# The first convolution block at 512 columns with single k-tiles first, attention's two roundings in another order, and a copy of the last gate/up block's transposed products

## The chip, the cores and the metric

The kernel runs on one core of a Trainium2 chip. The metric is device time in microseconds of that core for one execution; a smaller number is better. The core has a matrix engine, TensorE (PE), three engines for element work, VectorE (DVE), ScalarE (ACT) and GpSimd (POOL), and SyncE (SP), which here only issues transfers. The engines have an instruction stream each and wait for one another through semaphores. Transfers are issued by SP, ACT or POOL and run on 16 DMA engines. TensorE writes into PSUM, a small memory apart from SBUF, which the other engines read from.

## The reference

One layer of a hybrid block for 256 rows of 2048 numbers, all in float32. `x` is normalized, a single projection of 5120 columns gives the queries, keys and values of four attention heads and the two inputs of a convolution branch, both branches are joined and projected, and a SwiGLU network follows:

```python
xn = rms_norm(h, norm1_g[l])
proj = jnp.einsum('bsd,dn->bsn', xn, w_in[l])
q, k, v, ga, gg = jnp.split(proj, ...)                  # 1024 columns each
q = apply_rope(rms_norm(q, q_norm_g[l]), cos, sin)      # and k likewise
att = diff_attention(q, k, v, lam)                      # softmax 0 - lam * softmax 1, block-causal
att = rms_norm(att, subln_g[l]) * (1.0 - lambda_init)
u = ga * jax.nn.sigmoid(gg)
u = causal_depthwise_conv(u, conv_w[l], conv_b[l])      # 1024 channels, 31 taps
u = jax.nn.silu(layer_norm(u, conv_ln_g[l], conv_ln_b[l]))
mixed = jnp.concatenate([att, u], axis=-1)
h = h + jnp.einsum('bsm,md->bsd', mixed, w_out[l])
hn = rms_norm(h, norm2_g[l])
a = jnp.einsum('bsd,df->bsf', hn, w_gate[l])            # 5632 columns
bu = jnp.einsum('bsd,df->bsf', hn, w_up[l])
h = h + jnp.einsum('bsf,fd->bsd', jax.nn.silu(a) * bu, w_down[l])
```

## The kernel before, in words

**Operands.** The 256 rows are two row tiles of 128 (`m`), and the 2048 input columns of a projection are 16 k-tiles of 128. Every float32 operand is split in two: a high part rounded to the matrix engine's narrower type (`lhi`, `whi`, made on ACT) and what is left over (`llo`, `wlo`, made on DVE). A product is then three matmuls, high times high (L377), low part of the rows times high part of the weights (L378), and high part of the rows times low part of the weights (L383). The gate, up and down projections go the same way (L1085 to L1087, L1106, L1107 and L1111), most of them in a scheme that computes seven block products in place of eight.

**Chunks.** Weights come in chunks of 1024 numbers for each of 128 partitions, 512 KB: as a rule two k-tiles of a block of 512 columns, or four k-tiles of a block of 256 columns. SP loads a chunk as `raw` (`load_chunk`, L329), ACT casts `whi` (`round_chunk`, L338), DVE subtracts `wlo` (`split_chunk`, L347), and PE multiplies (`multiply`). For some chunks the low part is made without DVE: ACT writes minus `raw`, and a transfer issued by POOL adds the weights to it in flight (`wlo` at L341 and L342, or `lod` at L333 and L334 in `minus_chunk`). The planner `run_chunks` (from L466) writes the code chunk by chunk. Before the multiplication of chunk t it emits loads, casts and subtractions of the chunks that follow, as far ahead as the constants `AHEAD`, `ROUND_AHEAD` and `MINUS_AHEAD` say. The order of the code is the order in each engine's stream. `before` is a table of things to emit ahead of a chunk's load: transfers of the transposed input (`x_load`, L157), of the plain input (`h_load`, L517), and the constants.

**Beside the chunks.** Work that comes after a block is a generator, which is resumed twice for every chunk, and whose `yield` and `lag(n)` set how many half chunks lie between its steps. `room` and `held` count the four PSUM buffers called `aux` that these generators share; the blocks' sums have four of their own (`acc`). The convolution's taps are a queue by themselves (`side`): each half chunk emits as many taps (L593, one multiply-add on DVE of 128x256) as a credit of 1.30 us allows, out of which other work on DVE is paid too.

**Order of the work.** (1) At the start 19 transposes of an identity keep PE busy (`warm_up`), ACT issues the transfers of the gains (`cols`, a table with one row for each partition) and of the first two k-tiles of `x`, SP those of weights and of the rest. `x_part` makes `lhi` and `llo` for each k-tile of `x` by `split_scaled` (L239 on ACT, L240 on DVE), scaled with the gain of that k-tile. (2) The convolution's blocks come first: two of 256 columns (one channel tile of 128 with its gate), then three of 512 columns. The first block's chunks follow the parts of `x` (`XPARTS`, here 2, 2, 4, 4 and 4 k-tiles). The third block's sums lie in two buffers of the `aux` set (`spare`). After each of them `glu_done` waits for the row norms (`normed`, out of `h`), takes the sigmoid on ACT, makes `u` on DVE, transposes it on PE (`ps_u`), copies it to `upad` on ACT and puts 30 taps for each channel tile in the side queue. (3) Keys, queries and values follow, with `qk_rows` and `attend_scores` beside them (`p` at L767 is scaled by `a`, which POOL makes at L758 from a reciprocal of DVE's). `v_done` copies the values out of PSUM (L791), and `attend_values` makes for each of four heads `ps_o` on PE, `att` on ACT (L818), the transposes `ps_at` on PE (L826) and then `mahi` and `malo` for both column halves. (4) When all taps of four channel tiles are done, `conv_back` transposes them (`ps_y`, L614), copies them back, and, after the second half, normalizes them on ACT and transposes again (`ps_ln`, L652). (5) The output projection, which reads `mahi`, `malo` and the convolution's parts. (6) The SwiGLU network in three groups of gate/up blocks with their down blocks. After a gate/up block `transposed` (from L932) transposes the products, 256 columns at a time, to `ps_a` (L917), and makes high and low parts of them (L948 on ACT, L950 on DVE). After the last such block, number 10, come the down blocks of the last group, which read its parts.

## Time and profile before

| | |
|---|---|
| median of 3 runs | 1044.78 us (1044.53 to 1044.81) |
| the profiled execution's own time | 1043.19 us |
| its span in the trace | 1041.0 us |
| PE busy | 1030.0 us, 4739 instructions |
| PE's weight loads busy | 854.7 us |
| DVE busy | 864.5 us, 1088 instructions |
| ACT busy | 685.1 us, 865 instructions |
| POOL busy | 157.4 us, 197 instructions |
| granted TensorE clock | 1.0 |
| moved by DMA | 258.06 MB, mean 248 GB/s |

The span runs from the first to the last recorded event; the execution's own time is 2.2 us longer. Busy time is the time in which an engine worked on an instruction; weight loads (PEld) go beside matmuls. Matmuls are pipelined and their ends are modelled, so the rows of single matmuls overlap: from one start to the next is their real step. A row of the timeline gives the time from the start of the span, the busy time, the engine, the line in the code, the operation, output and inputs, shapes, the count of like instructions in a row, and in brackets the idle time before it with what ended it. In the list of waits stand the engine that waited, for which instruction, on whom, and then the total, the number of waits and the longest.

### The profile page before, as it was taken

The numbers are of one execution on the slowest core, as the hardware profiler recorded it, in microseconds if no ns is written. First come the engines' busy times: TensorE is split into PE (matmuls) and PEld (weight loads), VectorE is DVE, ScalarE is ACT, GpSimd is POOL, SyncE is SP. The second block draws the span as 40 slices with busy tenths as digits, with TensorE's granted clock in tenths as the row PEclk, the third lists the DMA queues.
The fourth block names the chain that finished last, engine by engine and source line by source line (L and its number), as shares of the span: only waits on it lengthen the run. The fifth ranks groups of instructions, "written<-read, shape, count | busy, mean of one in ns | idle before, by whom it ended". The sixth has DMA issues, their size and how long they took to land.

```text
span 1041.0 us, 13235 instructions
## 1 busy us (share of the span) xinstructions
PE 1030.0 (99%) x4739; PEld 854.7 (82%) x4739; DVE 864.5 (83%) x1088; ACT 685.1 (66%) x865; POOL 157.4 (15%) x197
## 2 busy tenths in 40 slices
PE   8999999999999999999999999999999999999998
PEld 8888888887788888788888888888888888888786
DVE  5799989996546599999979689998896697998983
ACT  6855567857756567777656567776765666767661
POOL 0130134322110101011002120110101121001121
PEclk9999999999999999999999999999999999999999
DMA  9776867675566669898889998987979999889896
GB/s 361 277 205 227 258 184 205 197 206 155 188 182 233 227 217 284 232 328 241 260 238 294 269 308 265 306 236 245 303 201 270 306 272 327 236 249 301 241 252 134
DMA packets 65346, 258.06 MB, mean 248 GB/s; under 512 B 7424, under 2 KB 8448, under 8 KB 57856
## 3 DMA queue, kind: packets, MB, share of 16 engines
q1 hardware_dynamic: 48224, 201.34, 53.4%
q0 software_dynamic: 16768, 55.58, 28.0%
q8 instruction: 37, 0.61, 0.2%
q10 hardware_dynamic: 288, 0.29, 0.1%
q14 instruction: 29, 0.24, 0.1%
HBM read 248.80 MB, written 8.39 MB: 247 GB/s over the span
## 4 chain that ended last, share of the span: by engine, by line
PE 94%; ACT 2%; DVE 1%; issue 1%; DMA 1%; POOL 1%; SPq 0%; DVEq 0%; ACTq 0%
PE q L1106 11%; PE q L1107 11%; PE q L1111 11%; PE acc L383 11%; PE acc L378 11%; PE acc L377 11%; PE q L1085 9%; PE q L1087 8%; PE q L1086 8%; PE ps_a L917 1%; DMA raw<-in_wts_dram 1%; ACT whi L338 1%; PE ps_s L728 1%; PE ps_h L854 0%; PE ps_qk L713 0%
## 5 line engine op out<-in xcount | busy, mean ns | idle before, releaser
L338 ACT CAST whi<-raw 128x1024 fp32r<-128x1024 f32 (+1 forms) x261 | 270.7, 1045 | 105.7 <-PE acc L378 46.3
L347 DVE TENSOR_TENSOR wlo<-raw,whi 128x1024 fp32r<-128x1024 f32 (+1 forms) x173 | 209.4, 1216 | 76.5 <-ACT whi L338 76.5
L377 PE MATMUL acc<-whi,lhi 128*128 128x512 f32 (+1 forms) x448 | 167.4, 379 | 1.6 <-ACT whi L338 1.2
L378 PE MATMUL acc<-whi,llo 128*128 128x512 f32 (+1 forms) x448 | 165.7, 375 | 0.9 <-DVE llo L240 0.9
L1068 DVE TENSOR_TENSOR wl<-wt,wh 128x2048 fp32r<-128x2048 f32 x58 | 132.6, 2287 | 20.1 <-ACT wh L1063 20.1
L1059 ACT CAST wh<-wb 128x1536 fp32r<-128x1536 f32 x58 | 86.0, 1483 | 87.1 <-PE q L1086 42.8
L342 POOL DMA_DIRECT2D wlo<-in_wts_dram x74 | 65.0, 889 | 510.7 <-ACT wlo L341 482.6
L1106 PE MATMUL q<-whi,chi 128*128 128x512 f32 x320 | 124.7, 390 | 0.0
L1107 PE MATMUL q<-whi,clo 128*128 128x512 f32 x320 | 124.6, 389 | 0.0
L1063 ACT CAST wh<-wt 128x2048 fp32r<-128x2048 f32 x58 | 110.4, 1904 | 18.6 <-DVE wt L1054 18.6
L1085 PE MATMUL q<-wh,fhi 128*128 128x512 f32 x280 | 109.1, 390 | 0.4 <-DVE sum L1190 0.4
L1087 PE MATMUL q<-wl,fhi 128*128 128x512 f32 x280 | 109.0, 389 | 0.0
L1086 PE MATMUL q<-wh,flo 128*128 128x512 f32 x280 | 108.9, 389 | 0.0
L1067 DVE TENSOR_TENSOR wl<-wb,wh 128x1536 fp32r<-128x1536 f32 x58 | 101.6, 1751 | 2.1 <-ACT wh L1059 2.1
L593 DVE SCALAR_TENSOR_TENSOR y<-upad,cw,y 128x256 f32<-128x256 f32 x240 | 101.9, 484 | 0.6 <-ACT y L586 0.4
L383 PE MATMUL acc<-wlo,lhi 128*128 128x512 f32 (+1 forms) x404 | 101.9, 377 | 0.0
L377 PEld LDWEIGHTS acc<-whi,lhi 128*128 128x128 f32 x448 | 84.4, 188 | 17.1 <-ACT whi L338 1.6
L378 PEld LDWEIGHTS acc<-whi,llo 128*128 128x128 f32 x448 | 84.4, 188 | 16.0 <-DVE llo L240 1.1
L1111 PE MATMUL q<-wlo,chi 128*128 128x512 f32 x320 | 86.9, 393 | 0.0
L383 PEld LDWEIGHTS acc<-wlo,lhi 128*128 128x128 f32 x404 | 71.5, 189 | 12.7
L341 ACT ACTIVATE wlo<-raw 128x1024 fp32r<-128x1024 f32 x74 | 78.1, 1056 | 0.0
L1052 DVE TENSOR_TENSOR wt<-wb 128x1024 f32<-128x1024 f32 x58 | 70.8, 1220 | 0.8 <-DMA wb<-in_wts_dram 0.4
(216 smaller groups left out, 1733.1 us busy)
## 6 DMA issues: line engine op xcount, KB each, us to landing
raw<-in_wts_dram SPq DMA_DIRECT2D x259, 512.0 KB, 5.8
wb<-in_wts_dram SPq DMA_DIRECT2D x57, 1024.0 KB, 8.1
wlo<-in_wts_dram POOLq DMA_DIRECT2D x74, 512.0 KB, 9.5
lod<-in_wts_dram POOLq DMA_DIRECT2D x14, 512.0 KB, 6.9
out_dram<-sum POOLq DMA_DIRECT2D x22, 256.0 KB, 7.0
h<-in_x_dram SPq DMA_DIRECT2D x4, 512.0 KB, 9.5
out_dram<-h POOLq DMA_DIRECT2D x8, 256.0 KB, 3.7
xt<-in_xt_dram SPq DMA_DIRECT2D x3, 512.0 KB, 7.3
```

The lines of the kernel that those rows point to most:

```text
L338: act.copy(c["hi"], c["raw"])
L347: dve.tensor_tensor(c["lo"], c["raw"], c["hi"].bitcast(F32), ALU.subtract)
L377: pe.matmul(ps[m], xhi[:, ms], hi[:, j, :], start=c["first"] and j == 0, stop=False)
L378: pe.matmul(ps[m], xlo[:, ms], hi[:, j, :], start=False, stop=False)
L383: pe.matmul(ps[m], xhi[:, ms], lo[:, j, :], start=False, stop=c["last"] and j == nk - 1)
L1068: dve.tensor_tensor(c["lo"][:, :4], c["t"], c["hi"][:, :4].bitcast(F32), ALU.subtract)
L1085: pe.matmul(ps, fhi[:, f, p, :], c["hi"][:, w], start=bool(first), stop=False)
L1086: pe.matmul(ps, flo[:, f, p, :], c["hi"][:, w], start=False, stop=False)
L1087: pe.matmul(ps, fhi[:, f, p, :], c["lo"][:, w], start=False, stop=bool(last))
L1106: pe.matmul(ps, plain[i][0][:, ms], hi[:, i, :], start=i == 0 and bool(c["first"].get(qs[m])), stop=False)
L1107: pe.matmul(ps, plain[i][1][:, ms], hi[:, i, :], start=False, stop=False)
L1111: pe.matmul(sum_bank(c, qs[m]), plain[i][0][:, ms], lo[:, i, :], start=False, stop=i == 1 and bool(c["last"].get(qs[m])))
```

## The change

There are five edits.

First, the convolution's blocks are four of 512 columns, where two of 256 and three of 512 columns stood. `XPARTS` has nine parts, of 1, 1 and seven times 2 k-tiles, so the first block's nine chunks are two of one k-tile (256 KB) and seven of two. No block's sums lie in the `aux` buffers any more, and `spare` leaves `glu_done`.

Second, the gains lie in the rows of the transposed input: each partition's row begins with its 58 gains, then come the 16 k-tiles. ACT's first transfer, `head`, brings the gains and k-tile 0 together, its second brings k-tile 1, and POOL copies the gains into `cols`. The parts of k-tiles 0 and 1 are scaled by gains read from `head`. `head` lies in the memory of `lod`.

Third, what stands around it moves: 17 warm-up transposes for 19, transfers of `h` from the load of the sixth chunk on (`H_FROM`) between those of `x`, late constants behind the load of the eleventh, and the count from which `minus_chunk` is used begins at 8 for 12, as the first block has more chunks.

Fourth, `attend_values` emits both roundings `mahi` on ACT and then both `malo` on DVE, where the code had `mahi` and `malo` of one column half ahead of those of the other, and two half chunks lie between `att` and the transposes for one. `v_done` begins one half chunk sooner.

Fifth, for gate/up block 10 `transposed` first copies the transposed products from PSUM into a tile `ac` on ACT, and both parts are made from the copy.

On SP at the start of the program, before, weights (`raw`) and parts of the transposed input (`xt`) alternate, and the plain input (`h`) follows behind all of `xt`. From the fourth load of weights to the constants:

```order
L329 DMA raw<-in_wts_dram 128x1024
L157 DMA xt<-in_xt_dram 128x1024
L329 DMA raw<-in_wts_dram 128x1024
L517 DMA h_81<-in_x_dram 128x1024
L329 DMA raw<-in_wts_dram 128x1024
L517 DMA h_82<-in_x_dram 128x1024
L329 DMA raw<-in_wts_dram 128x1024
L517 DMA h_81<-in_x_dram 128x1024
L329 DMA raw<-in_wts_dram 128x1024
L517 DMA h_82<-in_x_dram 128x1024
L329 DMA raw<-in_wts_dram 128x1024 x2
```

Now each `xt` is half as large, and the transfers of `h` stand between the last of them. The last two of each, to the constants:

```order
L159 DMA xt<-in_xt_dram 128x512
L521 DMA h_81<-in_x_dram 128x1024
L333 DMA raw<-in_wts_dram 128x1024
L159 DMA xt<-in_xt_dram 128x512
L521 DMA h_82<-in_x_dram 128x1024
L333 DMA raw<-in_wts_dram 128x1024 x5
L180 DMA cw<-in_conv_w_dram 128x248
L182 DMA gb<-in_vecs_dram 128x256
```

The ninth load of weights is the first of the last row of `raw` in both pieces, and all of `xt` and `h` stands ahead of it before as after. What moved is `h`, in between the last parts of `xt`, and the constants, which stand behind the tenth load of weights before and behind the thirteenth now.

On DVE at the start, before, low parts of `x` come two or four at a time between those of the weights:

```order
L240 SCALAR_TENSOR_TENSOR llo<-xt,cols,lhi 128x256 x2
L347 TENSOR_TENSOR wlo<-raw,whi 128x512 x2
L240 SCALAR_TENSOR_TENSOR llo<-xt,cols,lhi 128x256 x2
L347 TENSOR_TENSOR wlo<-raw,whi 128x1024
L240 SCALAR_TENSOR_TENSOR llo<-xt,cols,lhi 128x256 x4
L347 TENSOR_TENSOR wlo<-raw,whi 128x1024
L240 SCALAR_TENSOR_TENSOR llo<-xt,cols,lhi 128x256 x4
L347 TENSOR_TENSOR wlo<-raw,whi 128x1024
```

Now one each for the first two chunks (`head` holds k-tile 0 and the gains), and then two:

```order
L244 SCALAR_TENSOR_TENSOR llo<-head,lhi 128x256
L351 TENSOR_TENSOR wlo<-raw,whi 128x512 x2
L244 SCALAR_TENSOR_TENSOR llo<-xt,head,lhi 128x256
L351 TENSOR_TENSOR wlo<-raw,whi 128x1024
L244 SCALAR_TENSOR_TENSOR llo<-xt,cols,lhi 128x256 x2
L351 TENSOR_TENSOR wlo<-raw,whi 128x1024
L244 SCALAR_TENSOR_TENSOR llo<-xt,cols,lhi 128x256 x2
L351 TENSOR_TENSOR wlo<-raw,whi 128x1024
```

On ACT where attention's values of the first two heads are done, before: `att` of head 0, its two `mahi`, `att` of head 1, a cast of weights, and `mahi` of head 1.

```order
L818 ACTIVATE att<-ps_o,ro 128x256 x2
L239 ACTIVATE mahi<-ps_at,cols 128x256 x2
L818 ACTIVATE att<-ps_o,ro 128x256 x2
L338 CAST whi<-raw 128x1024
L239 ACTIVATE mahi<-ps_at,cols 128x256 x2
L767 ACTIVATE p_2555<-pr,a_2491 128x128
L767 ACTIVATE p_2557<-pr,a_2495 128x256
L338 CAST whi<-raw 128x1024
```

Now `att` of head 1 comes ahead of the roundings of head 0, and a cast stands between `att` and `mahi` of either:

```order
L820 ACTIVATE att<-ps_o,ro 128x256 x2
L342 CAST whi<-raw 128x1024
L820 ACTIVATE att<-ps_o,ro 128x256 x2
L832 ACTIVATE mahi<-ps_at,cols 128x256 x2
L342 CAST whi<-raw 128x1024
L832 ACTIVATE mahi<-ps_at,cols 128x256 x2
L770 ACTIVATE p_2441<-pr,a_2379 128x128
L770 ACTIVATE p_2443<-pr,a_2383 128x256
L342 CAST whi<-raw 128x1024
```

From the gate and up projections on, the streams of all engines are the same but for the copies. On ACT at the last gate/up block, before:

```order
L1063 CAST wh<-wt 128x2048
L948 CAST lhi<-ps_a 128x512
L338 CAST whi<-raw 128x1024
L341 ACTIVATE wlo<-raw 128x1024
L948 CAST lhi<-ps_a 128x512
L1059 CAST wh<-wb 128x1536
L338 CAST whi<-raw 128x1024 x2
```

Now a copy stands ahead of each cast, and the cast reads the copy:

```order
L1072 CAST wh<-wt 128x2048
L955 COPY ac<-ps_a 128x512
L957 CAST lhi<-ac 128x512
L342 CAST whi<-raw 128x1024
L345 ACTIVATE wlo<-raw 128x1024
L955 COPY ac<-ps_a 128x512
L957 CAST lhi<-ac 128x512
L1068 CAST wh<-wb 128x1536
L342 CAST whi<-raw 128x1024 x2
```

No other row moved there; DVE's low parts, in the same places as before, read `ac`. What moved is the moment at which `ps_a` is read for the last time: at DVE's low part before, at ACT's copy now.

The diff:

```diff
--- before.py
+++ after.py
@@ -49,18 +49,20 @@
 
 NK = 2
 
-WARM = 19
-
-XPARTS = (range(0, 2), range(2, 4), range(4, 8), range(8, 12), range(12, 16))
-
-CONV_BLOCKS = (1, 1, 2, 2, 2)
+WARM = 17
+
+XPARTS = (range(0, 1), range(1, 2)) + tuple(range(k, k + 2) for k in range(2, 16, 2))
+
+CONV_BLOCKS = (2, 2, 2, 2)
+
+H_FROM = 5
 
 AHEAD = 2
 ROUND_AHEAD, MINUS_AHEAD = 3, 5
 RAW_BUFS = 4
 AUX = 4
 
-MINUS_FROM = 12
+MINUS_FROM = 8
 
 LAG = (3, 2, 6)
 HL_BUFS = 4
@@ -113,7 +115,7 @@
 def tile_block(
     ctx: ExitStack,
     tc: tile.TileContext,
-    x, xt, conv_w, gains, vecs, rope, wts, out, placed_at,
+    x, xt, conv_w, vecs, rope, wts, out, placed_at,
 ):
     nc = tc.nc
     PSUM = bass.MemoryType.PSUM
@@ -155,10 +157,12 @@
         i, k = divmod(ks[0], HK)
         n = len(ks)
         queue.dma_start(out=halves_of_x[i][:, k : k + n].rearrange("p k s -> p (k s)"),
-                        in_=xt[:, ks[0] * S : (ks[0] + n) * S])
-
-    act.dma_start(out=cols, in_=gains)
-    x_load(XPARTS[0], act)
+                        in_=xt[:, NR + ks[0] * S : NR + (ks[0] + n) * S])
+
+    head = pre.tile([P, NK * N], F32, tag="lod", name="head", bufs=1)[:, : NR + S]
+    act.dma_start(out=head, in_=xt[:, : NR + S])
+    x_load(XPARTS[1], act)
+    pool.tensor_scalar(cols, head[:, :NR], 1.0, 0.0, ALU.mult, ALU.add)
 
     act.copy(small.tile([P, 8], F32, tag="rsq", name="first"), neghalf)
 
@@ -522,7 +526,8 @@
     def x_part(ks):
         for k in ks:
             xT[k] = lhs_pair("x", k)
-            split_scaled(xT[k], halves_of_x[k // HK][:, k % HK], col("g1", k))
+            src = halves_of_x[k // HK][:, k % HK] if k else head[:, NR:]
+            split_scaled(xT[k], src, col("g1", k) if k > 1 else head[:, AT["g1"] + k : AT["g1"] + k + 1])
 
     def x_rest():
         for part in XPARTS[1:]:
@@ -554,7 +559,7 @@
         pool.memset(upad[b][:, :, : W - 1], 0.0)
     y = pre.tile([P, NCT, S], F32, tag="y", name="y", bufs=1)
 
-    def glu_done(c0, nct, ps, spare):
+    def glu_done(c0, nct, ps):
 
         w = nct * P
         while not normed:
@@ -570,8 +575,6 @@
             u = pre.tile([P, HN], F32, tag="wt", name="u", bufs=4)
             dve.scalar_tensor_tensor(u[:, :w], ps[m][:, w:], rstd1[m], sig[m][:, :w], ALU.mult, ALU.mult)
             us.append(u)
-        if spare:
-            held[0] -= NM
         spend(0.25)
         yield from lag(4 if c0 == 0 else 3)
         yield from room(1)
@@ -786,7 +789,6 @@
         wTs[hd] = wT
 
     def v_done(b, ps):
-        yield
         for m in range(NM):
             act.activation(v_sb[m][:, b * N : (b + 1) * N], ps[m], AF.Copy, scale=rstd1[m])
         yield
@@ -818,16 +820,19 @@
             act.activation(at_, o[:, m, :], AF.Copy, scale=r[:, m : m + 1])
             atts.append(at_)
         held[0] -= 1
-        yield
+        yield from lag(2)
         yield from room(1)
         pt = aux_ps.tile([P, 2, S], F32, tag="aux", name="ps_at")
         for e in range(2):
             for m in range(NM):
                 pe.transpose(pt[:, e, m * P : (m + 1) * P], atts[m][:, e * P : (e + 1) * P], ident)
-        for e in range(2):
-            mixa[2 * hd + e] = lhs_pair("a", 2 * hd + e) if hd >= 2 else tuple(
-                pre.tile([P, S], F32R, tag=t, name=t, bufs=4) for t in ("mahi", "malo"))
-            split_scaled(mixa[2 * hd + e], pt[:, e, :], col("sg", e))
+        pairs = [lhs_pair("a", 2 * hd + e) if hd >= 2 else tuple(
+            pre.tile([P, S], F32R, tag=t, name=t, bufs=4) for t in ("mahi", "malo")) for e in range(2)]
+        for e, (hi, _) in enumerate(pairs):
+            act.activation(hi, pt[:, e, :], AF.Copy, scale=col("sg", e))
+        for e, (hi, lo) in enumerate(pairs):
+            dve.scalar_tensor_tensor(lo, pt[:, e, :], col("sg", e), hi.bitcast(F32), ALU.mult, ALU.subtract)
+            mixa[2 * hd + e] = hi, lo
         spend(-0.9)
 
 
@@ -945,6 +950,10 @@
                 yield from pair_forms(j, t, pt)
             else:
                 hi, lo = d["at"][j, t]
+                if j == FF // N - 1:
+                    a = ffn["pool"].tile([P, 2, S], F32, tag=f"sum{2 * t}", name="ac")
+                    act.copy(a, pt)
+                    pt = a
                 act.copy(hi, pt)
                 yield from lag(3)
                 dve.tensor_tensor(lo, pt, hi.bitcast(F32), ALU.subtract)
@@ -1253,8 +1262,8 @@
     c0 = 0
     for nct in CONV_BLOCKS:
         block("w_in", [(GC + c0 * P, nct * P), (AC + c0 * P, nct * P)], range(KD), fx,
-              lambda ps, c0=c0, nct=nct: glu_done(c0, nct, ps, c0 == 2),
-              cuts=[len(p) for p in XPARTS] if c0 == 0 else (), spare=c0 == 2)
+              lambda ps, c0=c0, nct=nct: glu_done(c0, nct, ps),
+              cuts=[len(p) for p in XPARTS] if c0 == 0 else ())
         c0 += nct
     for b in range(2):
         block("w_in", KC + b * N, range(KD), fx, lambda ps, b=b: qk_done("k", b, ps))
@@ -1284,12 +1293,13 @@
             down_block(g, n)
         j0 += nb
 
-    for c, part in enumerate(XPARTS):
+    for c, part in enumerate(XPARTS[2:], 2):
         before[c] = lambda part=part: x_load(part, sp)
     before[0] = lambda: (x_part(XPARTS[0]), start(x_rest()))
     for i in range(2 * NM):
-        before[len(XPARTS) + i] = lambda i=i: h_load(i)
-    before[len(XPARTS) + 2 * NM] = lambda: start(late_constants())
+        x_first = before.get(H_FROM + i, lambda: None)
+        before[H_FROM + i] = lambda i=i, x_first=x_first: (x_first(), h_load(i))
+    before[len(XPARTS) + 1] = lambda: start(late_constants())
     run_chunks()
 
 
@@ -1306,7 +1316,8 @@
     given = {name: np.asarray(inputs[name]).reshape(shape) for name, shape in _FLAT.items()}
     given["xt"] = given["x"].reshape(S, KD, P).transpose(2, 1, 0).reshape(P, KD * S)
     given["conv_w"] = np.asarray(inputs["conv_w"]).reshape(W, NCT, P).transpose(2, 1, 0).reshape(P, NCT * W)
-    given["gains"] = np.concatenate([np.asarray(inputs[name]).reshape(n, P) for name, _, n in ROWS]).T
+    gains = np.concatenate([np.asarray(inputs[name]).reshape(n, P) for name, _, n in ROWS]).T
+    given["xt"] = np.concatenate([gains, given["xt"]], axis=1)
     given["vecs"] = np.concatenate([np.asarray(inputs[name]).reshape(1, DH) for name in VECS])
     given["rope"] = rope_constants()
     total = sum(a * b for a, b in _WEIGHTS.values())
```

## The prediction

> **What bounds the kernel now.** The page of the profiled execution comes first: its span, the engines' busy time, and the clock granted to the matrix engine in 40 slices.
>
> ```profile
> span 1041.0 us, 13235 instructions
> PE 1030.0 (99%) x4739; PEld 854.7 (82%) x4739; DVE 864.5 (83%) x1088; ACT 685.1 (66%) x865; POOL 157.4 (15%) x197
> PEclk9999999999999999999999999999999999999999
> ```
>
> TensorE is busy for 99% of the span at a full clock. Time can come only from matmuls that are fewer or shorter, or from the few waits left on PE. The view of who waited for whom, for PE alone, lists those (total, times, longest):
>
> ```profile
> PE ps_warm L147 <- POOL neghalf L141: 1.4, 1, 1.4
> PE acc L377 <- ACT whi L338: 1.2, 1, 1.2
> PE ps_a L917 <- DVE llo L950: 1.1, 1, 1.1
> PE acc L378 <- DVE llo L240: 0.9, 1, 0.9
> PE ps_at L826 <- ACT att L818: 0.6, 1, 0.6
> PE acc L377 <- ACT v L791: 0.4, 1, 0.4
> PE ps_ln L652 <- DVE llo L240: 0.4, 1, 0.4
> PE acc L377 <- ACT lhi L239: 0.4, 1, 0.4
> PE ps_at L826 <- DVE malo L240: 0.3, 1, 0.3
> PE ps_y L614 <- DVE y L593: 0.2, 1, 0.2
> ```
>
> They sit in three places: the start (`whi`, `llo`, `lhi`), the stage where attention ends and the convolution is normalized (`ps_at`, `v`, `ps_ln`, `ps_y`), and the transposes of the last gate/up block (`ps_a`). The change touches all three. The timeline at the start shows PE's first product, its two waits, the steps of 256-column matmuls, the first 512-column one, and what ACT and DVE did for the ninth weight chunk (DVE's row at 11.28 shows how it makes low parts of `x`):
>
> ```profile
> 6.91 0.39 PE L377 MATMUL acc<-whi,lhi 128*128 128x256 f32 x1 [1.24 <-ACT whi L338]
> 10.56 0.38 PE L377 MATMUL acc<-whi,lhi 128*128 128x256 f32 x1 [0.36 <-ACT lhi L239]
> 11.81 0.39 PE L378 MATMUL acc<-whi,llo 128*128 128x256 f32 x1 [0.87 <-DVE llo L240]
> 11.28 1.67 DVE L240 SCALAR_TENSOR_TENSOR llo<-xt,cols,lhi 128x256 fp32r<-128x256 f32 x4
> ...
> 28.09 1.12 PE L383 MATMUL acc<-wlo,lhi 128*128 128x256 f32 x8
> 29.05 0.28 PE L377 MATMUL acc<-whi,lhi 128*128 128x256 f32 x1
> 31.93 0.40 PE L377 MATMUL acc<-whi,lhi 128*128 128x512 f32 x1
> ...
> 22.91 1.05 ACT L338 CAST whi<-raw 128x1024 fp32r<-128x1024 f32 x1 [2.23 <-DMA raw<-in_wts_dram]
> 25.49 1.05 ACT L338 CAST whi<-raw 128x1024 fp32r<-128x1024 f32 x1 [1.53 <-DMA raw<-in_wts_dram]
> 26.57 1.23 DVE L347 TENSOR_TENSOR wlo<-raw,whi 128x1024 fp32r<-128x1024 f32 x1 [1.35 <-ACT whi L338]
> ```
>
> The last gate/up block, on PE and DVE:
>
> ```profile
> 981.58 0.40 PE L1085 MATMUL q<-wh,lhi 128*128 128x512 f32 x1
> 986.12 0.39 PE L1087 MATMUL q<-wl,lhi 128*128 128x512 f32 x1
> 987.58 0.66 PE L917 MATMUL ps_a<-ident,sum 128*128 128x128 f32 x4 [1.07 <-DVE llo L950]
> 991.06 0.39 PE L1107 MATMUL q<-whi,llo 128*128 128x512 f32 x1
> 984.64 2.28 DVE L1068 TENSOR_TENSOR wl<-wt,wh 128x2048 fp32r<-128x2048 f32 x1
> 986.84 0.68 DVE L950 TENSOR_TENSOR llo<-ps_a,lhi 128x512 fp32r<-128x512 f32 x1
> 990.03 0.68 DVE L950 TENSOR_TENSOR llo<-ps_a,lhi 128x512 fp32r<-128x512 f32 x1
> ```
>
> From 981.58 to 986.12 stand 20 steps, 0.227 us each, though each row is drawn 0.39 long: an idle time in the wait table costs about 0.16 us more than it shows. A 256-column matmul steps at (29.05 - 28.09) / 8 = 0.120.
>
> **The start.** The two blocks of 256 columns took from 6.91 to 31.93: 192 x 0.120 = 23.0 us of work and 2.0 of waits. Now 96 matmuls of 512 columns do it, 96 x 0.227 = 21.8, so 1.2 us less work. The first chunk needs one k-tile of `x` instead of two, and gains and that tile come in one transfer, so PE can begin near 5.2, where 17 warm-up transposes end. That is 27.0 without any wait, 29.0 with as many as before: 2.9 us earlier.
>
> But the transfers do not move so far. The ninth weight chunk was cast at 25.49, waiting for its DMA. Ahead of it on the queues stood the eight weight chunks before it, all of `x` (2 MB), all of `h` (2 MB) and the gains. In the new order the same bytes stand ahead of the ninth chunk: I keep 25.49. There it held no one up, since PE still had five chunks of narrow matmuls queued; now it is the last chunk of the first block. From it: cast 1.05, then on DVE `wlo` from 26.57 to 27.8, then one `llo` of `x`, which stands behind it in DVE's order (some 0.45 of the 1.67 for four), to 28.25; 11 matmuls are left, 2.5 us, to 30.75. Against 31.93 that is **1.2 us earlier**, the value I take. The ends are 2.9 (transfers hide) and 0.5 (transfers later, second rival). Early waits for `llo` are inside this: PE gets over them before the ninth chunk.
>
> At nothing I put: two fewer warm-ups (PE waited 1.24 after them), the copy of the gains on POOL (only two clears of `upad` stand behind it, wanted after 40 us), the squares of `h` and the sigmoid (the next block covers them by 21 us), the freed PSUM pair of the third block, and the earlier first chunk whose low part a DMA makes (as many such chunks as before).
>
> **The attention stage.** Rows of ACT, POOL and DVE there, and DVE's busy time from 125 to 250 us:
>
> ```profile
> 236.87 0.47 ACT L239 ACTIVATE mahi<-ps_at,cols 128x256 fp32r<-128x256 f32 x1 [0.55 <-DVE malo L240]
> 237.24 0.83 ACT L818 ACTIVATE att<-ps_o,ro 128x256 f32<-128x256 f32 x2
> 236.35 0.48 DVE L240 SCALAR_TENSOR_TENSOR malo<-ps_at,cols,mahi 128x256 fp32r<-128x256 f32 x1 [3.62 <-ACT mahi L239]
> ...
> 233.39 0.33 POOL L758 TENSOR_TENSOR a<-r,neg_lam 128x1 f32<-128x1 f32 x2
> 247.45 2.43 POOL L758 TENSOR_TENSOR a<-r,neg_lam 128x1 f32<-128x1 f32 x2 [13.73 <-DVE r L756]
> 247.35 2.34 DVE L347 TENSOR_TENSOR wlo<-raw,whi 128x1024 fp32r<-128x1024 f32 x2
> sum 125.00, DVE 112.60; mean DVE 22.52
> 41.38 1.53 DVE L593 SCALAR_TENSOR_TENSOR y<-upad,cw,y 128x256 f32<-128x256 f32 x3 [0.44 <-ACT y L586]
> ```
>
> Before, ACT's second `mahi` waits 0.55 for DVE's first `malo`, and `att` of the next head, which PE's transposes need, stands behind both. The new order puts both roundings first, `att` ahead of them, and one more step before the transposes. So `ps_at` behind `malo` (0.3), `ps_at` behind `att` (0.6) and `ps_ln` behind `llo` (0.4) have their cause removed: 1.3 of idle and 3 x 0.16, together 1.8. The other two, `v` (0.4) and `ps_y` (0.2), I keep. What is late next is `att` of the last head, now behind the four normalizations of `upad`, and `wlo` of the first chunk of the output projection, with more taps ahead of it on DVE: 0.3 for them. Net **1.5**. The ends are 2.7 (all five go: 1.9 + 5 x 0.16) and 0 (each is replaced).
>
> On `v`: ACT's copies stand behind `p`, and that behind POOL's `a`, 2.43 us for a pair beside two `wlo`, 0.33 elsewhere. In the new order three taps follow the reciprocal on DVE instead of the two `wlo`. By the rows alone `a` may take either; I leave the wait. [...]
>
> **The last block.** A copy on ACT frees the PSUM buffer, so the second transposes no longer wait for DVE's `llo`: PE would do them at 986.35 instead of 987.58. DVE's own order stays: `llo` of the first half is done at 987.52, of the second at 990.71. PE's next chunk starts at 986.75, waits for 987.55 with its second matmul, and ends near 990.0; the one after wants the second `llo` at 990.25 and has it at 990.77, against 991.06 before. So **0.3** of 1.2 stays; the ends are 0 and 1.2. ACT has room for two copies of about 0.6, as it waited 2 us for these transposes.
>
> **Sum.** 1.2 + 1.5 + 0.3 = 3.0 us. The profiled execution took 1043.19 (2.2 around the span) and becomes 1040.2; the median of the runs shown is 1.6 higher, 1044.78, and becomes 1041.8. A measurement of this kernel can tell about 0.2%, 2.1 us, from no change.
>
> **Rivals.** *All covers hold*: transfers hide, every wait goes: 2.9 + 2.7 + 1.2 = 6.8, 1038.0. For it: the casts show a wait for DMA only from 22.91 on. Against it: the bytes ahead of the ninth chunk. 12%.
>
> *The transfers of `x` get slower.* The gains now stand at the front of each partition's row, so each 2 KB piece of `x` starts 232 bytes off. Between 22.91 and 25.49 one load of `h` and one chunk landed: 1.29 us per 512 KB. [...] Pieces of `x` that start so do not occur in this trace. 18%. [...]
>
> *The waits of attention move.* Start 1.2, last block 0.3, attention 0: 1043.3. For it: three engines hand over to each other there. Against it: two of the removed waits are plain order on ACT. 15%.
>
> *Slower: the taps become late.* The convolution's first taps start at 41.38; now only after a whole 512-column block and six chunks of 2.7 us, 30.75 + 16.3 = 47, so about 6 us of DVE work move back. PE's `ps_y` waits for the last tap. DVE has 125 - 112.6 = 12.4 us idle before it; if less than about 6 of that can be used, the rest becomes a wait of PE. At worst, with 1 us used, 5 of wait less 1.5 of gain: 1048.3. Against it: only 3.62 of the idle time is a wait ahead of which no tap can move. 5%.
>
> **Numbers.** The forecast has 50%: 1041.8, by itself 1040.5 to 1043. From 1038.8 to 1043.8 lie the forecast, the slow transfers, the moved waits and the near part of the first rival. Faster by over 0.2% (below 1042.7): the 50, 12, and about 10 of the 18: 0.72. Within: 0.23. Slower: 0.05.
>
> **What would show it.** First product near 5.2; first matmul of the second block near 30.75, right behind an `llo` after the ninth cast at about 25.5; the list of PE's waits without `ps_at` behind `malo` or `att` and without `ps_ln`; `ps_a` unstopped, but a wait for `llo` of 0.3 to 0.5 in each of the next two chunks. A ninth cast before 24.5 speaks for the first rival, after 26 for the second; a `ps_y` wait above 2 us for the fourth. A stall on PE between 50 and 225 us, where none stands now, would break the sum.

## The result, and the profile after

The median of six executions is 1040.81 us (1039.38 to 1041.07), that of six of the kernel before 1044.80 (1043.69 to 1045.41). The ratio is 0.9962, with a 95% interval from 0.9952 to 0.9972: 4.0 us less, between 2.9 and 5.0. The forecast was 1041.8, within 1038.8 to 1043.8. The execution traced after took 1041.07 us, near the upper end of its six, and the one traced before 1043.19, below all six beside it here; so the two traces lie only 2.1 us apart, and 1.8 in their spans.

The page after has the same look as before:

```profile
span 1039.2 us, 13042 instructions
PE 1030.1 (99%) x4641; PEld 850.3 (82%) x4641; DVE 862.3 (83%) x1086; ACT 685.6 (66%) x864; POOL 155.4 (15%) x198
```

PE is busy for as long as before with 98 instructions fewer: the waits shrank, and so should the work. That it did not is the first thing to explain. The view of who waited for whom, for PE, after:

```profile
PE acc L381 <- ACT lhi L243: 1.4, 1, 1.4
PE ps_warm L149 <- POOL neghalf L143: 1.4, 1, 1.4
PE acc L382 <- DVE llo L244: 0.7, 1, 0.7
PE q L1116 <- DVE llo L959: 0.6, 2, 0.4
PE q L1094 <- DVE sum L1199: 0.4, 1, 0.4
PE acc L387 <- DVE wlo L351: 0.2, 1, 0.2
```

All five waits of the attention stage are gone (`ps_at` twice, `v`, `ps_ln`, `ps_y`). The wait of 1.1 for `ps_a` has become two for `llo` (L959) in the chunks behind it. At the start one wait for `whi` went, and `lhi` grew from 0.4 to 1.4. New is also a wait of 0.2 for a `wlo`, near 165 us, in the part where the forecast wanted no stall.

The timeline of the start: PE's first product, the two waits, PE at half speed, the second block's first matmul, and the ninth chunk on ACT and DVE.

```profile
5.38 0.61 PE L381 MATMUL acc<-whi,lhi 128*128 128x512 f32 x1
9.91 0.50 PE L381 MATMUL acc<-whi,lhi 128*128 128x512 f32 x1 [1.36 <-ACT lhi L243]
11.16 0.50 PE L382 MATMUL acc<-whi,llo 128*128 128x512 f32 x1 [0.74 <-DVE llo L244]
13.26 1.91 PE L387 MATMUL acc<-wlo,lhi 128*128 128x512 f32 x4
14.96 0.63 PE L381 MATMUL acc<-whi,lhi 128*128 128x512 f32 x1
29.02 0.39 PE L381 MATMUL acc<-whi,lhi 128*128 128x512 f32 x1
31.74 0.39 PE L381 MATMUL acc<-whi,lhi 128*128 128x512 f32 x1
...
25.41 1.05 ACT L342 CAST whi<-raw 128x1024 fp32r<-128x1024 f32 x1 [1.36 <-DMA raw<-in_wts_dram]
27.64 0.88 DVE L244 SCALAR_TENSOR_TENSOR llo<-xt,cols,lhi 128x256 fp32r<-128x256 f32 x2
```

The four matmuls from 13.26 to 14.96 step at 0.43 us where 0.23 is usual. The view by windows of this stretch, whose columns are the length, PE's busy time, the granted clock, and DMA:

```profile
12.40:16.00 3.60, 3.60 (x10) 0.53 1.01 375
```

The granted clock is 0.53 over these 3.6 us, which makes 8 steps longer by 0.2, 1.6 us; a slice of 26 us on the page still shows a 9. This is why PE is busy for as long as before. The trace before has no such stretch.

At the other end of the front part, the first product of the gate and up projections (`q`), before and after:

```profile
389.26 0.39 PE L1106 MATMUL q<-whi,chi 128*128 128x512 f32 x1
```

```profile
387.01 0.39 PE L1115 MATMUL q<-whi,chi 128*128 128x512 f32 x1
```

And DVE's last two additions, ahead of the last output, before and after:

```profile
1037.28 0.76 DVE L1240 TENSOR_TENSOR sum<-q,sum 128x256 f32<-128x256 f32 x2 [0.60 <-PE q L1111]
```

```profile
1034.92 0.76 DVE L1249 TENSOR_TENSOR sum<-q,sum 128x256 f32<-128x256 f32 x2 [0.60 <-PE q L1120]
```

So the two traces part as follows. Start: 31.93 to 31.74, 0.2 less. Attention (second block to `q`): 357.33 to 355.27, 2.1 less. From `q` to the last additions: 648.02 to 647.91, 0.1 less. From there to the end of the span, 1041.0 and 1039.2: 3.7 to 4.3, 0.6 **more**. Together 1.8.

### The profile page after: what moved, and what is told of

Same layout as the page of the kernel before. It is cut to its first block, busy times and chain, and to the rows that moved or that the text cites. A ratio compares the mean times of both kernels' runs of the same rounds, so it can differ in the third digit from the quotient of the medians.

```text
span 1039.2 us, 13042 instructions
## 1 busy us (share of the span) xinstructions
PE 1030.1 (99%) x4641; PEld 850.3 (82%) x4641; DVE 862.3 (83%) x1086; ACT 685.6 (66%) x864; POOL 155.4 (15%) x198
## 4 chain that ended last, share of the span: by engine, by line
PE 95%; DVE 2%; ACT 1%; issue 1%; DMA 1%; POOL 0%; SPq 0%; DVEq 0%
PE q L1116 11%; PE q L1120 11%; PE q L1115 11%; PE acc L387 11%; PE acc L382 11%; PE acc L381 11%; PE q L1094 9%; PE q L1096 8%; PE q L1095 8%; PE ps_a L922 1%; DMA raw<-in_wts_dram 1%; PE ps_s L731 1%; PE ps_o L809 0%; DVE y L596 0%; PE ps_h L859 0%
## 5 line engine op out<-in xcount | busy, mean ns | idle before, releaser
L381 PE MATMUL acc<-whi,lhi 128*128 128x512 f32 x416 | 164.7, 396 | 1.5 <-ACT lhi L243 1.4
L382 PE MATMUL acc<-whi,llo 128*128 128x512 f32 x416 | 162.8, 391 | 0.7 <-DVE llo L244 0.7
L387 PE MATMUL acc<-wlo,lhi 128*128 128x512 f32 x368 | 101.4, 397 | 0.2 <-DVE wlo L351 0.2
L381 PEld LDWEIGHTS acc<-whi,lhi 128*128 128x128 f32 x416 | 78.5, 189 | 18.5 <-ACT lhi L243 1.8
L382 PEld LDWEIGHTS acc<-whi,llo 128*128 128x128 f32 x416 | 78.5, 189 | 17.3 <-DVE llo L244 1.2
L387 PEld LDWEIGHTS acc<-wlo,lhi 128*128 128x128 f32 x368 | 68.9, 189 | 14.6 <-DVE wlo L351 0.6
```

What stands on the lines that cost most here:

```text
L381: pe.matmul(ps[m], xhi[:, ms], hi[:, j, :], start=c["first"] and j == 0, stop=False)
L382: pe.matmul(ps[m], xlo[:, ms], hi[:, j, :], start=False, stop=False)
L387: pe.matmul(ps[m], xhi[:, ms], lo[:, j, :], start=False, stop=c["last"] and j == nk - 1)
```

## The experiments

Each run's traced execution gives the stages (us); ratios are against executions of the kernel before on the same chip.

| run | second block begins | from there to `q` | ratio to before, 95% interval |
|---|---|---|---|
| before, as forecast from | 31.93 | 357.33 | |
| before, again | 33.72 | 357.29 | 1.0002 (0.9992 to 1.0011) |
| start alone | 31.55 | 359.97 | 1.0000 (0.9990 to 1.0009) |
| attention alone | 32.23 | 357.07 | 0.9986 (0.9977 to 0.9995) |
| whole change | 31.74 | 355.27 | 0.9962 (0.9952 to 0.9972) |
| transposes as fill | 31.09 | 355.22 | 0.9963 (0.9951 to 0.9976) |
| x first | 30.12 | 355.22 | 0.9951 (0.9939 to 0.9964) |
| x first, h late | 28.25 | 357.16 | 0.9957 (0.9944 to 0.9969) |
| gains padded to 64 | 31.69 | 355.26 | 0.9965 (0.9952 to 0.9977) |
| without the copy | 32.05 | 355.32 | 0.9965 (0.9952 to 0.9979) |
| old order of roundings | 31.87 | 356.81 | 0.9983 (0.9974 to 0.9993) |
| one half chunk before the transposes | 30.66 | 357.92 | 0.9998 (0.9988 to 1.0007) |
| values copied later | 31.65 | 356.54 | 0.9973 (0.9964 to 0.9983) |
| x first, five transfers more | 29.58 | 357.08 | 0.9960 (0.9947 to 0.9974) |

**The kernel before, again** (no edit).

> The kernel before, unchanged, for the granted clock of more of its executions. In the profile of the change the granted clock fell to 0.53 from 12.4 to 16.0 us, which made 8 steps of 0.23 us into 0.43 us, 1.6 us in all, and every one of its six executions shows a mean clock of 0.998 or 0.999. The one execution of the kernel before that was traced shows 1.000 and took 1043.19 us, while the others took 1043.7 to 1045.4. Theory 'the change brought the slow stretch' (PE mostly idle from 8.4 to 11.2): executions of the kernel before show a clock of 1.000 throughout, and their times spread for another reason. Rival 'the slow stretch is in both': executions near 1044.8 us show 0.998 or 0.999, those near 1043.2 show 1.000, so that most of the 1.6 us between the traced execution and the median is this stretch.

Its traced execution shows the slow stretch too:

```profile
13.00:16.40 3.40, 3.40 (x18) 0.51 1.02 408
```

The second block begins 1.8 us later than in the first trace. So the stretch is no property of the change. An execution's mean clock tells of it: of the fourteen traces here, the seven with 0.999 or 1.000 have no stretch and the seven with 0.998 or less have one or two. But mean clock and time do not go together in this kernel's executions: of 27 beside this run, those with 1.000 took 1043.2 to 1045.2 and those with 0.998 1043.2 to 1045.2 (one with 0.996 took 1047.4). What else spreads them over 2 us is not settled; one transfer that came late in another trace (below) cost 1.5.

With the changed start they mostly do. In the changed kernel the executions with 0.998 took 1040.72 to 1041.07, those with 0.999 1039.38 to 1040.89; in three variants below (without the copy, old order of roundings, values copied later) the median of those with 0.998 lies 0.7 to 1.2 us above that of the others.

**The new start alone.** Attention's edits and the copy are taken out of the changed kernel.

> The changed start alone (blocks of 512 columns, nine parts of x, merged gains, 17 warm-ups, moved loads of h); attention and the last block as before. My forecast for this term was 1.2 us less time, bounded by the ninth chunk of weights. The profile of the whole change gives 0.2 us instead (second block's first matmul at 31.74 for 31.93), as 1.6 us of slow clock stand in it. If the slow stretch belongs to the change alone: 0.2 us less, about 1044.5, second block at 31.7, clock 0.998. If it is in the kernel before as well: 1.2 to 1.8 us less, 1043.0 to 1043.6. Rival 'start does nothing by itself, all of the gain is attention': no difference.

No difference at all, the rival's number, but not for its reason. The start is as early as in the whole change, even with the slow stretch in it; in this trace attention takes 2.6 us more than before. Its largest wait in the view for PE, and ACT's rows ahead of it:

```profile
PE ps_at L829 <- ACT att L821: 2.0, 1, 2.0
```

```profile
260.16 1.28 ACT L633 ACT_TABLE_LOAD   x1
262.50 0.83 ACT L821 ACTIVATE att<-ps_o,ro 128x256 f32<-128x256 f32 x2
263.22 1.52 ACT L645 ACTIVATE upad<-upad,lnb,lnr 128x512 f32<-128x512 f32 x2
268.78 1.52 ACT L645 ACTIVATE upad<-upad,lnb,lnr 128x512 f32<-128x512 f32 x2
270.20 0.82 ACT L821 ACTIVATE att<-ps_o,ro 128x256 f32<-128x256 f32 x2
```

Right behind that wait this trace has a second slow stretch:

```profile
270.90:274.40 3.50, 3.47 (x11) 0.51 0.98 215
```

It costs some 1.6 us like the first, so the stage without it is about 1.0 longer than before, not 2.6. This trace's mean clock is 0.996, which three of the run's eleven executions show; they took 1045.7 to 1045.9. The five with 0.999 or 1.000 took 1043.0 to 1043.6, where the 18 such executions of the kernel before have a median of 1043.8.

`att` of the last head, for which PE's transposes wait, stands behind the convolution's normalizations (L645). In the kernel before these rows stood at 257.65 and 260.38, ahead of the last two heads. They stand behind the taps in the order of the code, and the taps came later. The first taps of the kernel after, to be held against 41.38 in the prediction's row:

```profile
49.54 1.67 DVE L596 SCALAR_TENSOR_TENSOR y<-upad,cw,y 128x256 f32<-128x256 f32 x4 [5.32 <-ACT y L589]
```

They begin 8.2 us later, and the last tap ends 4.7 later (250.2 for 245.5).

**Attention's edits alone**, on the kernel before.

> The edits of attention alone on the kernel before (both high roundings ahead of both low ones, two half chunks between att and the transposes, values copied a half chunk sooner). My forecast for this term was 1.5 us less (ends 0 and 2.7). The profiles of the whole change show 2.0 less between the second block and the gate and up projections. Theory: the five waits at 237 to 267 us go here as well, 1.5 to 2.1 less, 1042.7 to 1043.3. Rival 'the new start's earlier taps and freed PSUM pair did it': under 0.7 less, and waits for ps_at or ps_ln stay.

1.5 us less (0.5 to 2.4) by the ratio. In the trace all five waits are gone, but a transfer of `lod`, issued at 59.6 and landed at 69.2, stopped PE once by 1.5 us; without that wait the stage took 355.6, 1.7 less than before.

**Three edits of attention, each undone in the changed kernel.**

```diff
-        for e, (hi, _) in enumerate(pairs): act.activation(hi, ...)
-        for e, (hi, lo) in enumerate(pairs): dve.scalar_tensor_tensor(lo, ...)
+        for e in range(2): split_scaled(mixa[2 * hd + e], pt[:, e, :], col("sg", e))
```

> The changed kernel with attention's old order of roundings (high and low part of one half, then of the other), the other two edits of attention kept. With the new start alone, attention took 2.6 us more than before (second block to gate and up projections 359.97 for 357.33), with the new start and all three edits 355.27. Theory 'the order of the roundings': each second mahi waits 0.55 us for the first malo again, att of the last head comes 0.6 us or more later, and the stage takes 1 to 3 us more than in the changed kernel. Rival 'the longer step before the transposes did it': no more than 0.3.

```diff
-        yield from lag(2)
+        yield
```

> The changed kernel with one half chunk between att and its transposes instead of two. Theory 'the longer step hides att': the waits of ps_at for att of 0.5 to 0.8 us near 237 and 264 us come back, 1 us more. Rival 'the order of the roundings and the earlier copy of the values bring att early enough': no more than 0.3.

```diff
     def v_done(b, ps):
+        yield
```

> The changed kernel with the copy of the values a half chunk later again. In the run of the new start alone the squares of the third head's values came at 259.15, with the whole change at 254.72, and so stood ahead of the activation's table load and the normalizations. Theory 'the earlier values let att of the last two heads slip ahead of the convolution's normalizations': att of the last head is late by 1.5 to 2.2 us again, and the stage takes 1 to 2.5 us more. Rival 'a half chunk of 1.3 us is hidden': no more than 0.3.

The stage takes 1.5, 2.7 (1 expected) and 1.3 us more, where the five traces that keep all three edits and the order of the transfers of `h` lie between 355.22 and 355.32 (the sixth, with five transfers more, has two waits of its own). Each of the three is needed; each rival of 0.3 falls. With the old order of roundings PE waited 0.7 for the last `att`, as expected, and 0.8 for a `wlo`, which I had not expected. Without the longer step PE waits for `att` at both places (total, times, longest):

```profile
PE ps_at L828 <- ACT att L820: 2.6, 2, 1.9
```

The values' later copy does not act as I said: PE waited 1.2 us for `lhi` and 0.7 for the `llo` behind it, for the third head's parts, not for `att`. The three losses sum to 5.5, and undoing all of them (the new start alone) cost 4.7, of which 1.6 is the second slow stretch: what one edit saves, another would in part have saved too.

**Nine transposes ahead of the third chunk.**

```diff
             part_of(t)
+            if t == 2:
+                warm_up(9)
             chunks[t]["multiply"](chunks[t])
```

> The changed kernel with nine more transposes of the identity on PE ahead of the third chunk, where PE is idle from 8.4 to 9.9 us; their result is not used. Theory 'idleness brings the slow stretch': the clock stays at 1.000, the steps between 12.4 and 16.0 us are 0.23, the second block begins near 30.5 (1.2 to 1.6 earlier, the ninth chunk's low parts then in the way), time 1039.3 to 1039.7. Rival 'the slow stretch comes from power or from the DMA load, not from idleness': it stays, time as the changed kernel, 1040.8, or some tenths more as the transposes delay the third chunk.

```profile
12.40:16.00 3.60, 3.60 (x17) 1.00 1.00 362
```

No slow stretch. The second block begins at 31.09, not 30.5, since each of the later chunks then waits some 0.4 for `llo`, which stands behind the chunk's low part on DVE. The executions took 1039.84 to 1040.31 and had a mean clock of 0.999; three of the changed kernel's six had 0.998. Over all runs: where the wait of 1.5 us ahead of the third chunk is filled or gone (this run and the three with x first), none of 20 executions shows 0.998 or less; in the five kernels with both early waits and none of 2 us in attention it is 16 of 36. So the stretch goes with the idle time. It does not go with the load of the DMA engines, whose share is 1.00 here and 1.01 in the trace after. Nor does it follow in every execution: the run with padded gains has the same two waits (1.46 and 1.02 over a step) and in its trace no stretch:

```profile
12.40:16.00 3.60, 3.60 (x17) 1.00 1.02 389
```

In the trace after, PE was idle for 2.1 of some 2.8 us (1.36 and 0.74 in the rows of the start) from 8.4 on, ahead of the stretch. What makes the clock fall in one execution and not in another, and what sets the length of the stretch, no run here shows.

**The gains padded to 64 columns**, so that parts of `x` begin at multiples of 256 bytes.

> The changed kernel with the gains padded from 58 to 64 columns, so that a row of gains takes 256 bytes and every piece of x begins at a multiple of that again. In the profile of the change a part of x took 0.66 us between two landings, where half of a weight chunk of 1.27 us would be 0.64. Theory 'the pieces that begin elsewhere cost nothing worth telling': parts of x take 0.64 to 0.66, time as the changed kernel, 1040.8. [...]

Same time, and parts of `x` land 0.66 to 0.68 us after the piece ahead of them, with 58 columns 0.65 to 0.67 (but for one part in either trace, 1.22 and 0.85). ACT's casts of the eighth and ninth chunk show it too, with one load of `h`, one chunk and one part of `x` between them: 3.22 us here, and 25.41 - 22.19 = 3.22 in the changed kernel.

```profile
23.05 1.05 ACT L342 CAST whi<-raw 128x1024 fp32r<-128x1024 f32 x1 [1.40 <-DMA raw<-in_wts_dram]
26.27 1.05 ACT L342 CAST whi<-raw 128x1024 fp32r<-128x1024 f32 x1 [1.36 <-DMA raw<-in_wts_dram]
```

The second rival falls: where the pieces of `x` begin has no effect that these rows show.

The ninth chunk's cast came 0.9 later here than in the changed kernel, and so the second block began at 31.69 without any slow stretch: PE waited for that chunk's `llo`.

**Each part of x ahead of its weight chunk.**

```diff
                 if t < len(XPARTS):
+                    if t == 0:
+                        part_of(0)
+                    if t + 1 < len(XPARTS):
+                        load_until(t + 2, True)
+                        x_part(XPARTS[t + 1])
                     until("part", part_of, t + 2)
```

(`x_rest` then only waits as long, and goes on with the squares of `h`.)

> The changed kernel with each part of x rounded and split ahead of the weight chunk that needs it; in the change it stands behind that chunk's cast on ACT and behind its low part on DVE. The transfers stay. Theory 'PE's early waits and the slow stretch that follows them hold the start': the third chunk begins near 9.45 and its second matmul no longer waits, no slow stretch, and then the ninth chunk's cast (25.4 + 1.05) is what is late: its matmuls begin near 26.5, the second block near 29.2 instead of 31.74, 2.5 us less than the changed kernel, 1038.0 to 1038.6. Rival 'the ninth chunk holds the start at my 30.75': 1.0 us less, 1039.8. Rival 'the slow stretch stays whatever PE waits': the second block near 30.8.

PE's waits in the first block:

```profile
6.23 0.50 PE L381 MATMUL acc<-whi,lhi 128*128 128x512 f32 x1 [1.49 <-ACT whi L342]
9.41 0.50 PE L381 MATMUL acc<-whi,lhi 128*128 128x512 f32 x1 [0.17 <-ACT whi L342]
20.83 0.50 PE L381 MATMUL acc<-whi,lhi 128*128 128x512 f32 x1 [0.23 <-ACT whi L342]
24.05 0.50 PE L381 MATMUL acc<-whi,lhi 128*128 128x512 f32 x1 [0.21 <-ACT whi L342]
27.27 0.50 PE L381 MATMUL acc<-whi,lhi 128*128 128x512 f32 x1 [0.20 <-ACT whi L342]
```

The third chunk begins where expected; no slow stretch; and now the seventh, eighth and ninth chunks wait for their casts, which begin 0.1 us after the landings of their transfers. The second block begins 1.6 us earlier than in the changed kernel (2.5 expected: the first product was 0.9 late in this execution, and the transfers of the last chunks came later). Median 1039.34, against 1040.86 and 1041.17 for the two variants beside it that keep the changed kernel's start. By its median it is the fastest version tried; the next run's interval overlaps.

**The same, with h loaded from the tenth chunk on.**

```diff
-H_FROM = 5
+H_FROM = 9
...
-    before[len(XPARTS) + 1] = lambda: start(late_constants())
+    before[H_FROM + 2 * NM] = lambda: start(late_constants())
```

(The late constants move behind the last load of `h` with it.)

> As the run before, with the four loads of h from the tenth chunk of weights on instead of from the sixth, so that only weights and x stand ahead of the ninth chunk. Theory 'bytes ahead of the ninth chunk set its time': the ninth cast comes near 20.5 instead of 25.4, PE has no wait after the third chunk, the second block begins near 28.5, 0.7 us earlier than in the run before, and the time is 1037.3 to 1037.9. What may eat it: the row norms come later (about 42 instead of 38 us), with them the taps of the first block, some 4 us. Rival 'later taps cost at attention': a wait for ps_y or for att comes back, and the time is the same as or above the run before.

The bytes do set the ninth chunk's time: its cast came at 19.73, and the second block began at 28.25. But attention took 357.16, 1.9 us more than in the run before, and the time stayed. A wait of 0.4 for `v` was back, and a longer one for `att`. That wait in the view for PE, and the two rows of ACT behind it:

```profile
PE ps_at L830 <- ACT att L822: 1.5, 1, 1.5
```

```profile
265.10 1.52 ACT L647 ACTIVATE upad<-upad,lnb,lnr 128x512 f32<-128x512 f32 x2
266.52 0.82 ACT L822 ACTIVATE att<-ps_o,ro 128x256 f32<-128x256 f32 x2
```

As with the new start alone, the last `att` stands right behind the normalizations, and PE is there before it. The rival holds.

**Without the copy of the last products.**

```diff
-                if j == FF // N - 1:
-                    a = ffn["pool"].tile([P, 2, S], F32, tag=f"sum{2 * t}", name="ac")
-                    act.copy(a, pt)
-                    pt = a
```

> The changed kernel without the copy of the last gate/up block's products. Forecast for the copy: 0.3 us of a wait of 1.2 goes, since DVE's low parts stay where they are. In the profile of the change, two waits of 0.63 and 0.35 stand where one of 1.23 stood. Theory: a single wait of 1.1 to 1.2 for llo at the transposes is back, 0.2 to 0.3 us more than the changed kernel. Rival 'the copy frees the buffer, and that is worth the whole wait': 1.0 more. Rival 'nothing': the same.

The single wait is back (1.24 over a step), and from `q` to PE's last matmul it takes 647.61 us, for 647.48 with the copy; the four other traces without it have 647.56 to 647.62. The other traces with it have 647.41 to 647.46, but for one of 647.81 (old order of roundings), where PE waited 0.8 instead of 0.4 for a `sum`. The copy is worth 0.15 us. The ratio can't tell that.

**Five transfers more.** SP loads the constants of the queries and keys in eight pieces instead of three.

```diff
-        for t, v in ((gb, vecs[:2]), (lamv, vecs[2:])):
-            sp.dma_start(out=t, in_=v...)
-        sp.dma_start(out=rt, in_=rope...)
+        for i in range(6):
+            t = gb[:, i : i + 1] if i < 2 else lamv[:, i - 2 : i - 1]
+            sp.dma_start(out=t, in_=vecs[i : i + 1]...)
+        for m in range(NM):
+            sp.dma_start(out=rt[:, m], in_=rope[m * P : (m + 1) * P])
```

> The kernel with each part of x ahead of its weight chunk, and with the constants of the queries and keys loaded in eight transfers instead of three (the same bytes), so that SP issues eight transfers more than the kernel before instead of three. In all eight traced executions with the new start the span ends 4.72 to 4.74 us after PE's last matmul begins, in the three with the old start 4.13 to 4.14, and at the end SP looks through eight queues one after the other. Theory 'where that search stands when the last output lands depends on the number of transfers, counted in eights': the end is 4.1 again, the span 0.6 shorter, 1038.7 for 1039.3. Rival 'the new start makes the end longer by something else': 4.7 again, time as the run without the five transfers or 0.1 more.

From PE's last matmul to the end of the span it took 4.21 us, for 4.73 without the five: the theory holds for most of the 0.6, in one trace. The time did not follow, since two waits were longer in this execution than in that of the run without the five: 1.0 for none for the cast of a chunk at 32 us, whose transfer now stands behind the small ones, and 1.0 for 0.3 at a `wlo` at 164 us.

## Why the forecast held, and where its steps were off

The sum said 3.0 us less on the traced execution's own time, 1040.2; traced after is 1041.07, and its six executions lie between 1039.38 and that. The two traces give 0.2, 2.1 and 0.1 less and 0.6 more where the sum had 1.2, 1.5, 0.3 and nothing. That the medians came out within 1.0 of the forecast is in part luck, as a spread of 2 us in the kernel before is in them that is not explained.

- **The start, 1.2: the mechanism held where no slow stretch fell in; 0.2 in this trace.** The ninth chunk was cast at 25.41, as kept (25.49). But in this trace PE came to it only at 29.02, when its parts were long there. Here the step "PE gets over them before the ninth chunk" failed: the wait for `lhi` was longer than before (1.5 us over a step, for 0.5; that for `llo` stayed, 1.0 for 1.1), and a stretch of half clock followed, for which the sum had no term. Three traces have this start and no stretch (transposes as fill, padded gains, one half chunk before the transposes). In each PE waits for the ninth chunk's `llo`, as forecast, and the second block begins 5.4 us after that chunk's cast, where the forecast had 5.3. The casts came at 25.69, 26.27 and 25.23, and the second blocks at 31.09, 31.69 and 30.66, for 30.75 in the forecast. The last of them:

```profile
25.23 1.05 ACT L342 CAST whi<-raw 128x1024 fp32r<-128x1024 f32 x1 [1.37 <-DMA raw<-in_wts_dram]
27.99 0.50 PE L382 MATMUL acc<-whi,llo 128*128 128x512 f32 x1 [0.21 <-DVE llo L244]
30.66 0.39 PE L381 MATMUL acc<-whi,lhi 128*128 128x512 f32 x1
```

  That is 1.3 less than in the trace before without a stretch (31.93), and 0.8 and 0.2 less in the other two, as the cast came later. With a stretch in both kernels it is 2.0 less (33.72 to 31.74). In the trace after, 25.41 and 5.4 would have made 30.8 without the stretch: of its 1.6 us some 0.9 count, and the rest lies where PE would have waited anyway. The early wait for `lhi` comes from order, not from bytes: on ACT the third chunk's cast stands ahead of the two k-tiles of `x`, and on DVE its low part stands ahead of theirs, though they had landed 1.9 us before the chunk. With that order turned on ACT and DVE, the `llo` no longer stands behind the ninth chunk's low part, and the last three chunks wait for their transfers alone. The low end of 0.5, with slower transfers of `x`, rests on a cost for pieces that begin 232 bytes off which no run shows: parts of `x` landed 0.65 to 0.67 us after the piece ahead of them so, and 0.66 to 0.68 from multiples of 256 bytes (but for one part in either trace).
- **Attention, 1.5: right in kind, with 2.1 measured.** Five waits of 2.7 went, and some 0.7 of small ones came, `att` of the last head among them as forecast. The wait for `v`, which I had kept, went too. The pair of `a` on POOL took 0.80 us beside a row of taps, for 2.43 beside two `wlo`:

```profile
249.08 0.80 POOL L761 TENSOR_TENSOR a<-r,neg_lam 128x1 f32<-128x1 f32 x2 [4.48 <-DVE r L759]
```

  Why the pair is shorter there, no run shows; and a short `a` is neither needed for `v` to come in time nor enough. With attention's edits alone `a` still took as long, and the wait for `v` was gone: the values' copy begins sooner, and ACT did it ahead of `qT`, no longer behind it.

```profile
248.79 2.43 POOL L758 TENSOR_TENSOR a<-r,neg_lam 128x1 f32<-128x1 f32 x2 [13.89 <-DVE r L756]
```

  With the new start alone and with the values copied later `a` took 0.80, and the wait was gone without the sooner copy. With x first and h late `a` took 0.80, and the wait was there. I had left the sooner copy, which is part of the change, out of this term.
- **What I had not seen in it:** on the new start the edits are worth 4.7 us in the traces, 3.1 without the second slow stretch, and on the old one 1.7. The fourth rival, late taps, was real: 8 us late where I had 6. It did not strike at `ps_y`, where I had looked, but through ACT's order at the last `att`: a wait of 2.0 and, in that trace, a slow stretch behind it. Attention's edits paid for it. The third rival, that the waits of attention only move, fell for the whole change.
- **The last block, 0.3: 0.15 measured.** The two later waits were 0.6 and 0.35 over a step, as forecast in place, and each brought a slower step behind it (0.34 and 0.33 us for 0.23).
- **The end, not in the sum: 0.6 more** in every trace with three more transfers on SP.

The gain of 4.0 in the medians is larger than 1.8 in the spans since the execution that I counted from was among the shortest of its kernel and the one traced after near the longest of its own: the first had no slow stretch, the second had one. By the mean clock a stretch falls into 23 of the 80 executions of the kernel before whose clock was recorded. The rest of the spread is open.

## What to carry to other kernels

An edit that makes one stage earlier also moves everything that is queued by count behind it; look where the moved work (here the taps, then the normalizations) now stands in the order of the engine that the last stage waits for, and test the parts alone and together, since here 0 and 1.5 alone made 4.0 together. Look at the granted clock of a stage before its length is put down to a wait: a wait of 2.0 us had 1.6 more behind it. Where a stage waits for two inputs, emit first the one that lands first. Traced executions of one kernel can differ by as much as the change: take stages from several.

## What was not expected of the hardware

- A stretch of some 3.4 us at a granted clock of about half (0.53 from 12.40 to 16.00 in the trace after, 0.51 from 13.00 to 16.40 in that of the kernel before, again) behind waits of PE of 1 to 2 us (1.36 and 0.74 after, 2.0 in the second stretch with the new start alone), in some executions of both kernels. It makes the steps in it longer by 1.6 us together. In the page's row of slices it cannot be seen; a mean clock of 0.998 or less is its sign here.
- The length of the program's end went with the count of transfers: 4.13 to 4.14 us from PE's last matmul in the three traces of the old start, 4.72 to 4.74 in ten with the new, 4.21 with five transfers more. In the traces before and after, SP there waits for the outputs' transfers and then for PE's sequencer (L1321 and L1332), 1.0 and 0.6 us in all before, 1.3 and 1.0 after. It goes through eight semaphores of transfers one after the other, 0.06 us a step where it does not wait: that of the last output is the eighth before and the third after, and the five steps behind it make some 0.3 of the 0.6. The rest is in the wait for PE's sequencer; why that one grew is not shown.
